# Hybrid encoder block: four of seven low weight parts of each output unit moved from GpSimd to VectorE

## The chip, the cores and the metric

One core of one Trainium2 chip. The metric is device time in microseconds. PE is TensorE (PEld its weight loads), DVE is VectorE, ACT is ScalarE, POOL is GpSimd, SP is the engine that issues most DMAs.

## The reference

One pre-norm mixer layer over x of 1024 tokens by 2048 columns, in float32. One input projection feeds two head groups, whose gated outputs are joined and mixed by one output projection:

```
h = rmsnorm(x, norm_w)
proj = einsum('bsd,de->bse', h, w_in)            # 2048 x 5632
q_a, k_a, v_a, g_a, q_r, k_r, v_r, g_r = split(proj)
attn = windowed_attention(q_a, k_a, v_a)         # +-128 tokens, 16 heads, 4 kv heads
attn = rmsnorm(attn, attn_out_norm_w) * silu(g_a)
ret  = bidirectional_retention(rotary(q_r), rotary(k_r), v_r)    # 8 heads, chunks of 128
ret  = head_groupnorm(ret, ret_gn_w) * silu(g_r)
mixed = concatenate([attn, ret])                 # 1024 x 2048
x = x + einsum('bse,ed->bsd', mixed, w_out)      # 2048 x 2048
return rmsnorm(x, final_norm_w)
```

## The kernel before

**Float32 products from rounded parts.** A float32 operand is held as two parts: `hi`, the value rounded to the matmul's float32r format, and `lo`, the value minus `hi`. Each product takes three matmuls: hi by hi, hi by lo, lo by hi. The helper `split` (L171 to L173) makes the parts: ACT writes `hi` (a rounding copy, L172), then another engine subtracts `hi` from the source (L173, recorded at L166, the line of the helper `tt`). With `G` that engine is POOL.

**Seven products in place of eight.** The output projection is done by the scheme of Strassen and Winograd on blocks. There are 16 output units (`NO`), numbered q = NF to NF + 15, after the NF = 16 units of the input projection that use the same scheme. A unit has seven products p = 0 to 6, each of four steps j with three matmuls of 128 by 512 (`multiply`, L1167 to L1169): 84 matmuls a unit. For these units the stationary operand, the pair `wh` and `wl`, is a 128 by 512 block of the mixed activations, and the moving operand, the rows `h`, is a combination of the output weights.

**Stages of four units.** The four units of a stage (o % 4, o = q - NF) share 28 rows, four for each product. When the last unit of a stage has finished a product, `o_rows` schedules the next stage's four rows for it: SP loads a row (L1035), ACT writes its high half (L1038), DVE its low half (L166, `h<-h`). So the rows change three times while the output units run.

**Raw blocks and sums.** A unit needs four raw blocks `raws[q, 0..3]`, loaded by SP from `xm` (L1133) into eight rotating buffers of tag `r`. `prep_sums` forms the Winograd sums on POOL (L166, `r<-r,r`), four operations a unit: part 0 turns raw block 0 into a difference and makes `sums[q]`, part 1 changes raw block 2, part 2 changes `sums[q]`. `prep(q, p)` then splits the block of a product: p = 0 and 4 take raw block 0, p = 1 block 1, p = 3 block 2, p = 5 block 3, p = 2 and 6 the sum. `wh` and `wl` have three buffers each.

**Order.** In this part each engine runs its instructions in the order of the program. A slot is one product; the slots of neighbouring units interleave as (q,0), (q,1), (q-1,6), (q,2), (q-1,5), (q,3), (q,4). In the middle of slot n, after its step j = 1, `between` calls `prep` for slot n + 2 and then work that was put off (`run_later`). `point`, after every step, issues row loads, row splits, retention steps and the final normalisation. At the end of a slot `o_collect` lets DVE add the product's PSUM bank to an SBUF tile (`e`, `y` or `t` in the profile, L166). The banks: products 0, 2, 5 and 4 of a unit accumulate into one of tag Ma, products 1, 3 and 6 use tag Mb; there are two Ma, two Mb, one O and three ST banks. Tag ST is handed out by `pS()` and `pT()`, which retention's transposes and small matmuls use in turn; the last pair of retention heads is still at work while the first output units run. From stage 2 on ACT squares each finished tile (L1474) and `finish` normalises and stores the rows: a small power on POOL, a few one-column operations on DVE (`newton`), four scalings on DVE (L169).

Of the kernel before, what the change touches and what calls it, by code (L numbers as in the profile page):

```python
# [10 lines left out]
F32R = mybir.dt.float32r  # L11
AF = mybir.ActivationFunctionType
ALU = mybir.AluOpType
# [20 lines left out]
NS, NF = len(STD), len(FAST)  # L34
# [5 lines left out]
def hybrid_block(ctx: ExitStack, tc: tile.TileContext, a: dict, out: bass.AP):  # L40
    nc = tc.nc
    ctx.enter_context(tc.manual_schedule(engines={mybir.EngineType.Pool}))
    V, A, G, T, SP = nc.vector, nc.scalar, nc.gpsimd, nc.tensor, nc.sync
# [94 lines left out]
    def wpair(i):  # L138
        return w_high(), w_low()
# [10 lines left out]
    def psum(tag, bufs):  # L150
        return ps.tile([128, 512], F32, tag=tag, name=nm("ps" + tag), bufs=bufs)

    def pS():
        return psum("ST", 3)
# [10 lines left out]
    def tt(eng, o, x, y, op):  # L165
        eng.tensor_tensor(o, x, y, op)  # L166
# [4 lines left out]
    def split(o_hi, o_lo, x, eng=None):  # L171
        A.copy(o_hi, x)  # L172
        tt(eng or V, o_lo, x, o_hi.bitcast(F32), ALU.subtract)  # L173
# [974 lines left out]
    def prep(q, p):  # L1148
        src = {0: 0, 1: 1, 3: 2, 4: 0, 5: 3}.get(p)
        src = sums[q] if src is None else raws[q, src]  # L1150
        hi, lo = wpair(q)
        split(hi, lo, src, G)
        ready_w[q, p] = (hi, lo)

    def place(q, p, j):
# [133 lines left out]
    for u, (kind, i) in enumerate(STD):  # L1289
# [5 lines left out]
        for pos in range(NK):  # L1295
# [24 lines left out]
            if last_u and pos == 7:  # L1320
                raw_room(0, (2, 0, 3, 1))
                for x in (0, 2, 3, 1):
                    raw_load(0, x)
            elif last_u and pos == 13:
                prep_sums(0, 0)
                prep_sums(0, 1)
            elif last_u and pos in (12, 14):
                prep(*slots[pos // 2 - 6])
            wh, wl = wsp[wi]
            first, last = pos == 0, pos == NK - 1  # L1330
            for b in range(4):
                p = plain[b]
# [56 lines left out]
    for n, (q, p) in enumerate(slots):  # L1389
        slot[0] = n  # L1390
        prepare(q, p, 0)

        def between():
            if n + 2 < len(slots):
                prep(*slots[n + 2])
            run_later()

        if not q:
            rows_done([("c", r) for r in range(4 * p, 4 * p + 4)])
        multiply(q, p, between)  # L1400
        collect(q, p)

        if q == LAST and p < 4:
            for r in range(4 * p, 4 * p + 4):
                todo.append((pt[0] + 2, ("x", r), r, xd[r]))
        if (q, p) == (LAST, 4):
            n_w[0] = W_ALL
            w_load(W_STD)
            w_load(W_STD + 1)
            w_load(W_STD + 2)  # L1410
        elif (q, p) == (LAST, 6):
            w_split(W_STD)
# [91 lines left out]
    def first_slots(w, b):  # L1504
        if (w, b) == (1, 0):
            top[0] = NF + NO
            raw_room(NF, (2, 0, 3, 1))
            for x in (0, 2, 3, 1):
                raw_load(NF, x)
        elif (w, b) == (3, 0):  # L1510
            for x in wanted.pop(-1):
                o_request(*x)
            prep(*oslots[0])
        elif (w, b) == (3, 1):
            prep_sums(NF, 0)
            prep_sums(NF, 1)
        elif (w, b) == (3, 3):
            prep(*oslots[1])

    for u, (kind, i) in enumerate(FAST):  # L1520
# [32 lines left out]
        for w in range(4):  # L1553
# [6 lines left out]
            for b in range(4):  # L1560
                et, hf = b // 2, b % 2
                p = whole[b]
# [159 lines left out]
```

## Time and profile before

| | |
|---|---|
| median of 3 runs | 1531.51 us (1528.52 to 1531.87) |
| profiled execution | 1533.07 us, span 1531.3 us, mean granted TensorE clock 0.994 |
| busy over the span | PE 1463.1, PEld 1218.4, DVE 922.0, ACT 660.4, POOL 844.6 us |
| output units | about 1156 to 1518 us, then 13 us to finish the last rows |
| wl by POOL, from 1156 us | 111 instructions, 1271 / 1300 / 2727 ns (least, median, most) |
| wh by ACT, from 1156 us | 111 instructions, 603 / 622 / 644 ns |
| DMA | 353.18 MB, mean 231 GB/s |

Busy times of different engines overlap. Matmuls are pipelined: one starts every 0.226 us though each is shown with about 0.39 us. A line such as `PE psMa L1168 <- DVE h L166: 7.2, 10, 0.7` reads: PE's instruction at L1168 that writes psMa waited in all 7.2 us, 10 times, at most 0.7 us, for DVE's instruction at L166 that writes h. Buffer numbers are left out of names.

### The profile page before, as it was taken

To read this page: it belongs to the slowest core of one execution; us is meant where nothing else is said; L and a number is where in the kernel's file an instruction comes from. 1 tells how busy PE (TensorE), PEld (TensorE's weight loads), DVE (VectorE), ACT (ScalarE), POOL (GpSimd) and SP (SyncE) were. 2 spreads that over 40 slices of the span, in tenths; PEclk is the share of its full clock that TensorE was granted. 3 is DMA by queue.
4 is the path that set the end of the run, shared out by engine and by line. 5 is a ranking of instruction groups with operands and counts; after the bars stand their busy time and mean duration, and the time that the engine had idled before them with its cause. 6 is when DMAs were issued, how large, how long until landed. Compare 5 with 4: busy or idle time off the path is not lost.

```text
span 1531.3 us, 22172 instructions
## 1 busy us (share of the span) xinstructions
PE 1463.1 (96%) x7250; PEld 1218.4 (80%) x7250; DVE 922.0 (60%) x1791; ACT 660.4 (43%) x1401; POOL 844.6 (55%) x641
## 2 busy tenths in 40 slices
PE   8999998999999999999999999999999998989985
PEld 6998886777888888888788888788887776868764
DVE  5573333864565565565424755754869868483986
ACT  5311133775676675776221232132244243354522
POOL 3232221245546655655666656566446677687863
PEclk9999999999999999999999999999999999999998
DMA  8879889986456456446888589497496586765654
GB/s 304 287 259 337 283 264 314 283 277 203 123 168 162 135 168 186 128 153 208 308 283 268 172 278 355 164 313 271 149 305 240 157 297 217 269 241 182 206 166 144
DMA packets 225072, 353.18 MB, mean 231 GB/s; under 512 B 31883, under 2 KB 86155, under 8 KB 223548
## 3 DMA queue, kind: packets, MB, share of 16 engines
q1 hardware_dynamic: 194492, 330.78, 65.5%
q10 hardware_dynamic: 30464, 20.98, 4.4%
q8 instruction: 57, 0.93, 0.2%
q14 instruction: 59, 0.48, 0.1%
HBM read 239.97 MB, written 124.29 MB: 238 GB/s over the span
## 4 chain that ended last, share of the span: by engine, by line
PE 71%; DMA 9%; DVE 7%; issue 6%; POOL 4%; ACT 2%; SPq 1%; ACTq 0%; DVEq 0%; POOLq 0%
PE psMa L1168 5%; PE psMa L1167 5%; PE psMa L1169 5%; PE psMb L1169 4%; PE psMa L1573 4%; PE psMb L1573 4%; PE psMb L1168 4%; PE psMb L1167 4%; PE psMb L1575 4%; PE psMb L1574 4%; PE psMa L1575 4%; PE psMa L1574 4%; DVE h L166 2%; DMA h<-wc 2%; PE psST L605 2%
## 5 line engine op out<-in xcount | busy, mean ns | idle before, releaser
L166 POOL TENSOR_TENSOR wl<-r,wh 128x512 fp32r<-128x512 f32 x288 | 393.2, 1369 | 400.7 <-ACT wh L172 380.1
L172 ACT CAST wh<-r 128x512 fp32r<-128x512 f32 x288 | 177.5, 619 | 304.2 <-PE psMa L1168 70.8
L1168 PE MATMUL psMa<-h,wh 128*128 128x512 f32 x512 | 201.9, 394 | 7.4 <-DVE h L166 7.2
L1167 PE MATMUL psMa<-h,wh 128*128 128x512 f32 x512 | 203.0, 397 | 4.2 <-DVE t L166 3.5
L1169 PE MATMUL psMa<-h,wl 128*128 128x512 f32 x512 | 200.9, 392 | 0.0
L166 DVE TENSOR_TENSOR h<-h 128x512 fp32r<-128x512 f32 x156 | 174.3, 1146 | 22.9 <-ACT h L1038 22.9
L166 POOL TENSOR_TENSOR r<-r,r 128x512 f32<-128x512 f32 x128 | 182.1, 1423 | 2.8
L166 POOL TENSOR_TENSOR wl<-e,wh 128x512 fp32r<-128x512 f32 x48 | 73.0, 1523 | 199.0 <-ACT wh L172 194.9
L1169 PE MATMUL psMb<-h,wl 128*128 128x512 f32 x384 | 151.4, 394 | 7.9 <-POOL wl L166 7.8
L1167 PE MATMUL psMb<-h,wh 128*128 128x512 f32 x384 | 151.9, 396 | 3.0 <-ACT e L1201 1.7
L1168 PE MATMUL psMb<-h,wh 128*128 128x512 f32 x384 | 150.8, 393 | 2.4 <-DVE h L166 2.3
L166 DVE TENSOR_TENSOR e<-psMa,e 128x512 f32<-128x512 f32 x86 | 58.8, 685 | 106.5 <-PE psMa L1575 79.5
L1168 PEld LDWEIGHTS psMa<-h,wh 128*128 128x128 f32 x512 | 96.6, 189 | 29.4 <-DVE h L166 12.8
L1167 PEld LDWEIGHTS psMa<-h,wh 128*128 128x128 f32 x512 | 96.5, 188 | 23.1 <-issue 3.7
L1169 PEld LDWEIGHTS psMa<-h,wl 128*128 128x128 f32 x512 | 96.5, 189 | 21.0 <-POOL wl L166 0.6
L1573 PE MATMUL psMa<-h,wh 128*128 128x512 f32 x256 | 104.0, 406 | 2.5 <-DVE e L166 2.5
L1573 PE MATMUL psMb<-h,wh 128*128 128x512 f32 x256 | 103.4, 404 | 0.0
L1575 PE MATMUL psMa<-h,wl 128*128 128x512 f32 x256 | 100.0, 391 | 0.0
L1038 ACT CAST h<-h 128x512 fp32r<-128x512 f32 x156 | 90.4, 616 | 22.4 <-DMA h<-cd 9.7
L1575 PE MATMUL psMb<-h,wl 128*128 128x512 f32 x256 | 100.0, 390 | 0.0
L1574 PE MATMUL psMa<-h,wh 128*128 128x512 f32 x256 | 99.8, 390 | 0.0
L1574 PE MATMUL psMb<-h,wh 128*128 128x512 f32 x256 | 99.8, 390 | 0.0
(268 smaller groups left out, 3282.8 us busy)
## 6 DMA issues: line engine op xcount, KB each, us to landing
h<-wc SPq DMA_DIRECT2D x112, 256.0 KB, 5.1
r<-in_w_fast SPq DMA_DIRECT2D x64, 256.0 KB, 3.1
r<-in_w_half SPq DMA_DIRECT2D x64, 256.0 KB, 4.7
h<-in_w_out SPq DMA_DIRECT2D x64, 256.0 KB, 5.0
e<-yd SPq DMA_DIRECT2D x64, 256.0 KB, 4.7
wc<-h SPq DMA_DIRECT2D x64, 256.0 KB, 4.5
r<-xm SPq DMA_DIRECT2D x64, 256.0 KB, 4.1
t<-in_xT SPq DMA_DIRECT2D x31, 512.0 KB, 5.9
```

Source lines behind the costliest of these rows:

```text
L166: eng.tensor_tensor(o, x, y, op)
L172: A.copy(o_hi, x)
L605: T.transpose(p[:, c0], x[:, c0], ident)
L1038: A.copy(rows[r][:, 0:512], rows[r][:, 512:1024].bitcast(F32))
L1167: T.matmul(bank, wh[:, ws], hh, start=(j == 0 and p in (0, 1, 3)), stop=False, skip_group_check=True)
L1168: T.matmul(bank, wh[:, ws], hl, start=False, stop=False, skip_group_check=True)
L1169: T.matmul(bank, wl[:, ws], hh, start=False, stop=(j == 3), skip_group_check=True)
L1573: T.matmul(p, wh[:, ws], hh, start=(w, kk) == (0, 0), stop=False)
L1574: T.matmul(p, wh[:, ws], hl, start=False, stop=False)
L1575: T.matmul(p, wl[:, ws], hh, start=False, stop=last)
```

## The change

In `prep`, for the output units (`q >= NF`) and the products 0, 4, 5 and 6, `split` on POOL is replaced. ACT still writes `hi`; it then writes the same rounded copy once more, into a PSUM bank `c` of tag ST; DVE subtracts `c` from the source and writes `lo`. Products 1, 2 and 3, and all units of the input projection, stay as they were.

```
@@ -1149,7 +1149,14 @@
         src = {0: 0, 1: 1, 3: 2, 4: 0, 5: 3}.get(p)
         src = sums[q] if src is None else raws[q, src]
         hi, lo = wpair(q)
-        split(hi, lo, src, G)
+        if q >= NF and p in (0, 4, 5, 6):
+
+            c = pS()
+            A.copy(hi, src)
+            A.copy(c.bitcast(F32R), src)
+            tt(V, lo, src, c, ALU.subtract)
+        else:
+            split(hi, lo, src, G)
         ready_w[q, p] = (hi, lo)
```

## The prediction

> **What bounds the kernel now.** I read the page first: its head, then the busy times by stage, the waits of TensorE, and the order of time at the places where it waits.
>
> ```profile
> span 1531.3 us, 22172 instructions
> PE 1463.1 (96%) x7250; PEld 1218.4 (80%) x7250; DVE 922.0 (60%) x1791; ACT 660.4 (43%) x1401; POOL 844.6 (55%) x641
> ```
>
> TensorE carries the time. The profiled execution took 1533.07 us, 1.6 us above the median of the runs (1531.51) and 1.8 us above its own span. The edit acts where q >= NF, in the output products, which run from 1156 us to the end. So I cut that part into stages (columns: window, length, busy time and instructions of each engine, clock, DMA share, GB/s).
>
> ```profile
> 1156.00:1250.00 94.00, 88.39 (x438) 72.37 (x437) 72.79 (x140) 36.41 (x72) 62.21 (x50) 0.98 0.62 202
> 1250.00:1292.00 42.00, 37.73 (x157) 28.58 (x156) 41.18 (x39) 19.33 (x35) 33.52 (x22) 1.00 0.78 267
> 1292.00:1330.00 38.00, 38.00 (x169) 31.48 (x168) 10.98 (x16) 10.80 (x18) 28.21 (x23) 1.00 0.69 214
> 1330.00:1372.00 42.00, 37.76 (x161) 29.35 (x160) 40.35 (x40) 22.32 (x43) 32.45 (x21) 1.00 0.79 287
> ...
> 1410.00:1450.00 40.00, 37.12 (x157) 28.58 (x156) 38.55 (x37) 25.70 (x52) 32.34 (x21) 1.00 0.70 243
> 1450.00:1518.00 68.00, 58.01 (x244) 44.53 (x242) 54.26 (x91) 19.56 (x44) 41.04 (x35) 1.00 0.47 151
> 1518.00:1531.00 13.00, 0.00 (x0) 0.00 (x0) 7.05 (x16) 0.72 (x2) 0.55 (x1) 0.64 0.49 162
> ```
>
> The quiet stage 1292 to 1330 is the yardstick: weight loads fill 31.48 of 38 us, 0.828 of the time, one matmul every 38/168 = 0.226 us, with DVE at 29%. Nothing is lost there, so a shorter POOL chain wins nothing there. By the same 0.828 the other stages lose: 1250 to 1292, 42 - 28.58/0.828 = 7.5 us; 1330 to 1372, 6.6; 1410 to 1450, 5.5; 1450 to 1518, 14.2. In the first three DVE is busy 96 to 98% of the time: they are the changes of the rows, when 28 new rows are split by DVE. 1156 to 1250 holds the last retention work, and 1518 to 1531 the last rows' finish, which this edit doesn't touch. The waits of TensorE and of its weight loads from 1156 to 1518 (total us, times, longest):
>
> ```profile
> PE psMa L1168 <- DVE h L166: 7.2, 10, 0.7
> PE psMb L1169 <- POOL wl L166: 6.6, 5, 1.6
> PE psMa L1167 <- DVE t L166: 3.5, 3, 2.0
> ...
> PEld psMa L1168 <- DVE h L166: 12.8, 13, 1.2
> PEld psMb L1169 <- POOL wl L166: 9.7, 7, 2.1
> ```
>
> So the rows' low parts on DVE come last most often, then POOL's low parts of the weights, then banks that DVE empties late.
>
> Why is DVE slow in a row change? The order of time there (start, length, engine):
>
> ```profile
> 1272.43 2.87 DVE L166 TENSOR_TENSOR h<-h 128x512 fp32r<-128x512 f32 x2
> 1275.21 0.68 DVE L166 TENSOR_TENSOR e<-psMb,e 128x512 f32<-128x512 f32 x1
> 1275.82 2.86 DVE L166 TENSOR_TENSOR h<-h 128x512 fp32r<-128x512 f32 x2
> ...
> 1273.32 1.42 POOL L166 TENSOR_TENSOR wl<-r,wh 128x512 fp32r<-128x512 f32 x1 [0.27 <-ACT wh L172]
> 1274.70 3.42 POOL L166 TENSOR_TENSOR r<-r,r 128x512 f32<-128x512 f32 x2
> ...
> 1275.35 0.50 PE L1168 MATMUL psMa<-h,wh 128*128 128x512 f32 x1 [0.73 <-DVE h L166]
> 1277.04 0.50 PE L1168 MATMUL psMa<-h,wh 128*128 128x512 f32 x1 [0.73 <-DVE h L166]
> ```
>
> TensorE moves on by one row every 1.69 us (1275.35 to 1277.04), which is one POOL operation and one DVE subtraction taken in turn. The spread of the durations in 1250 to 1292 (min/median/max ns) shows who suffers:
>
> ```profile
> L166 DVE TENSOR_TENSOR h<-h x26: 674/1604/1781, 1249.2 to 1290.6; 128x512 fp32r<-128x512 f32 x26
> L166 DVE TENSOR_TENSOR e<-psMa,e x7: 673/677/693, 1255.3 to 1291.8; 128x512 f32<-128x512 f32 x7
> L166 POOL TENSOR_TENSOR wl<-r,wh x14: 1291/1594/1782, 1248.9 to 1290.9; 128x512 fp32r<-128x512 f32 x14
> L166 POOL TENSOR_TENSOR r<-r,r x8: 1609/1740/1748, 1250.2 to 1284.0; 128x512 f32<-128x512 f32 x8
> ```
>
> A DVE subtraction with both inputs in SBUF takes 674 ns or up to 1781; one with an input in PSUM takes 673 to 693 whatever POOL does. That asymmetry decides what the change is worth.
>
> **The change part by part.** It takes 4 of 7 wl off POOL in each of 16 units: 64 instructions. It adds 64 copies on ACT into a bank of tag ST and 64 subtractions on DVE with one input in that bank. No DMA is added and no matmul changed.
>
> Prices of the new instructions, from their nearest rows:
>
> ```profile
> L166 DVE TENSOR_TENSOR PTl<-psST,PTh x128: 410/552/560, 266.6 to 705.1; 128x384 fp32r<-128x384 f32 x96, 128x256 fp32r<-128x256 f32 x32
> ...
> L1474 ACT ACTIVATE psO<-y x16: 602/602/604, 1345.6 to 1437.2; 128x512 f32<-128x512 f32 x16
> ...
> L172 ACT CAST wh<-r x111: 603/622/644, 1155.4 to 1508.6; 128x512 fp32r<-128x512 f32 x111
> ```
>
> The subtraction: same operation as PTl at 512 columns, and as e<-psMa at 677 ns; following ones start 0.60 to 0.61 us later (1275.21 to 1275.82), so I take 0.61 us of DVE each. The copy: between 0.60 (into PSUM) and 0.62 us (a cast); I take 0.60. It is 64 x 0.60 = 38 us of ACT, four in 19 us of a unit, hidden by ACT's idle half (19.33 of 42 us in the worst change of rows); without that cover each would delay the next wh by 0.60 us. The Trainium skill's "VectorE: DVE Perf Modes", section on the TRN2 errata, charges a PSUM source 120 cycles of fixed cost against 58, which would make each subtraction 0.065 us dearer than from SBUF and the sum 0.5 us worse per row change; here 677 against 674 ns shows no such step, and the row decides.
>
> *Row changes.* In 1250 to 1292 DVE is busy 41.18 us with 39 instructions that need 39 x 0.61 = 23.8: it waits 17.4 us for 22 POOL operations, 0.79 each. Four sevenths of the 14 wl leave, 8: -6.3. Eight subtractions come: +4.9. Net -1.4 us if waiting shrinks in proportion. The better end: 21 DVE instructions on PSUM (13 + 8, 12.8 us) run beside POOL's remaining 14 x 1.28 = 17.9 us, only 5.1 of which then meets an h: 17.4 - 5.1 - 4.9 = -7.4. The worse end: each new subtraction also waits for its second copy, 8 x 0.60, so +3.4. I take -3, nearer the proportional end because h is still most of DVE's work, and +1 for that waiting: -2 per change, three changes, -6. TensorE follows DVE one for one there, up to the 7.5, 6.6 and 5.5 us that it loses.
>
> *TensorE waiting for wl.* Of the 9.7 us, three waits (near 1344, 1471 and 1495 us, 2.1 + 1.7 + 2.0) stand in the first row of product 6, by the order of banks, and product 6 is moved. Its chain was POOL's sum, one cast, one POOL subtraction of 1.28 us plus queue; it becomes the sum, two casts, 0.61 us of DVE. The sum itself comes earlier, with fewer wl ahead of it on POOL. Ends: 0 (DVE is as late as POOL was) and -5.8; I take -2, since the sums still come from POOL.
>
> *Last stage.* DVE's tiny operations wait for POOL too, and a bank is then emptied late:
>
> ```profile
> 1456.46 1.24 DVE L166 TENSOR_TENSOR ft<-fv,fy 128x1 f32<-128x1 f32 x1 [0.68 <-POOL fy L166]
> 1457.74 1.22 DVE L166 TENSOR_TENSOR ft<-ft,fy 128x1 f32<-128x1 f32 x1
> ...
> 1456.40 2.54 POOL L166 TENSOR_TENSOR wl<-r,wh 128x512 fp32r<-128x512 f32 x2
> ...
> 1460.88 0.47 PE L1167 MATMUL psMa<-h,wh 128*128 128x512 f32 x1 [2.00 <-DVE t L166]
> ```
>
> The two wl at 1456.40 belong to products 4 and 0, both moved: 2 x 1.1 us of DVE waiting goes, 2 x 0.61 comes. DVE has room here (54.26 of 68 us, plus 12 x 0.61 = 7.3). Ends -3.5 (all of this wait) and +3; I take -0.5.
>
> *Retention overlap, 1156 to 1250.* Twelve subtractions, 7.3 us, join a DVE busy 72.79 of 94 us, and the extra bank shares three ST buffers with retention. A dozen wl of POOL leave. One wait stands there that DVE sets:
>
> ```profile
> 1176.13 0.49 PE L812 MATMUL psO<-ST,qs 128*128 128x128 f32 x2 [3.20 <-DVE ST L169]
> ...
> 1177.32 0.63 PE L1168 MATMUL psMa<-h,wh 128*128 128x512 f32 x1
> ...
> 1180.99 0.39 PE L1168 MATMUL psMa<-h,wh 128*128 128x512 f32 x1
> ```
>
> After that wait matmuls last 0.63 instead of 0.39 us for some 3.5 us, about 1.7 us lost. I take 0, ends -4 and +4. "TensorE: Matmul & The Clock Gate" of the Trainium skill, Part 1, says the array falls to half clock after an idle window of about 3.4 us. By that rule a slightly shorter wait here would save those 1.7 us as well, and the sum would be -10.2; the trace agrees that the slowing follows a wait of this size.
>
> *Waits that are added.* DVE's queue is in order. A new subtraction waits for ACT's copy, which stands behind the cast, which waits for its wh buffer; behind the subtraction stand the row splits and bank adds that TensorE waits for. SP is concerned too: it waits for wl before it reloads a raw buffer, and will wait for DVE instead for four of seven.
>
> ```profile
> ACT wh L172 <- PE psMa L1168: 46.6, 25, 5.1
> ...
> SPq L1133 <- POOL wl L166: 71.1, 29, 7.9
> ```
>
> ACT's wait ends when TensorE ends the product before, and DVE's own bank add waits for the same moment, so I expect the extra at one copy or less; SP at nothing, as the new subtraction ends within 0.7 us of the old one's time.
>
> Sum: -6 - 2 - 0.5 + 0 = -8.5 us; on the profiled execution 1533.07 to 1524.6, on the median 1531.5 to 1523.0.
>
> **The rivals.** *DVE's queue is blocked (slower).* Place: the row changes, 24 subtractions. If each holds the row splits behind it for w, the loss is 24 w. From w = 0.35 us it eats the 8.5; at w = 0.60, one copy, 14.4 - 8.5 = +6, so 1537.5. For it: DVE has no idle time there. Against it: rows for a product are put into DVE's queue ahead of the next subtraction, and ACT is half idle.
>
> *An even exchange (no change).* The -1.4 per row change is eaten by the waiting, and product 6 waits for DVE as it did for POOL: 1531. For it: the same DVE is the bound before and after.
>
> *Row changes become TensorE's (much faster).* With the better end of -7.4, capped by the losses, most of 19.6 us comes back, say 16, with 3 + 1 from the other places: 1511.5. For it: PSUM-fed work runs beside POOL untouched.
>
> **How the numbers follow.** Forecast, a gain of 3 to 16 us: 0.48. Much faster: 0.12. Even, within 0.2% (about 3 us, what a measurement of this kernel can tell from no change): 0.17. Slower: 0.23, mostly near 1537. Faster in all: 0.60. The range 1508 to 1538 takes in the two outer cases' centres; the likeliest case alone spans 1515 to 1528.5.
>
> **What would show it.** In the profile after, the median of h<-h at the row changes should fall from 1604 ns to 1300 or less; the new subtractions should last 0.67 to 0.69; TensorE's wait for POOL's wl should shrink from 9.7 us, and DVE's idle time ahead of the new wl stay small. I am wrong if DVE shows long waits for ACT ahead of wl in the row changes, if h<-h stays where it is, or if TensorE's waits for DVE's wl take the place of POOL's.

## The result and the profile after

The changed kernel takes 1520.14 us (median of 4 runs, 1517.61 to 1522.07) against 1531.36 us for the kernel before in the same comparison: ratio 0.993, interval 0.9909 to 0.995. The profiled executions have spans of 1519.2 and 1531.3 us, 12.1 us apart. In the lines below the seven added lines of code have moved line numbers: the three matmuls are L1174 to L1176, the new cast of the high part is L1155 and the copy into PSUM L1156.

The page after, its head and busy times:

```profile
span 1519.2 us, 22187 instructions
PE 1461.1 (96%) x7250; PEld 1219.6 (80%) x7250; DVE 923.3 (61%) x1855; ACT 690.8 (45%) x1465; POOL 751.4 (49%) x577
```

DVE has 64 instructions more and is busy for only 1.3 us more (923.3 against 922.0): its other instructions have become shorter by nearly as much as the new ones take. POOL lost 93.2 us, ACT gained 30.4. The stages (window, length, busy time and instructions of each engine, clock, DMA share, GB/s):

```profile
1156.00:1250.00 94.00, 87.21 (x441) 71.58 (x440) 75.43 (x157) 43.52 (x85) 45.92 (x37) 1.00 0.63 208
1250.00:1292.00 42.00, 41.41 (x179) 32.74 (x178) 38.22 (x48) 24.75 (x45) 22.32 (x15) 1.00 0.80 279
1292.00:1330.00 38.00, 38.00 (x169) 31.48 (x168) 18.08 (x28) 15.18 (x27) 17.62 (x14) 1.00 0.71 243
1330.00:1372.00 42.00, 38.95 (x163) 29.76 (x162) 36.85 (x44) 26.92 (x55) 21.50 (x14) 1.00 0.75 265
...
1410.00:1450.00 40.00, 38.48 (x164) 29.97 (x163) 37.36 (x49) 28.00 (x59) 20.63 (x14) 1.00 0.60 203
```

In the first row change TensorE's weight loads fill 32.74 us instead of 28.58, in the second 29.76 instead of 29.35, in the third 29.97 instead of 28.58. The quiet stage has the same 31.48 as before, as it had nothing to win. By the second row change the changed kernel is 5 us ahead, so that the later windows don't hold quite the same work in both kernels; the table of starts below doesn't have this fault. What the weight loads wait for from 1156 to 1518 us:

```profile
PEld psMa L1175 <- DVE h L166: 10.2, 13, 1.4
PEld psMb L1176 <- DVE wl L166: 3.2, 2, 2.4
...
PEld psMb L1175 <- DVE h L166: 2.4, 5, 0.7
...
PEld psMb L1176 <- POOL wl L166: 1.1, 1, 1.1
...
PEld psMa L1176 <- DVE wl L166: 0.8, 2, 0.6
```

The 9.7 us of waits for POOL's wl are down to 1.1, but 3.2 + 0.8 us of waits for DVE's wl have come. The waits for the rows that DVE splits fell from 12.8 + 5.1 to 10.2 + 2.4.

The first row change in groups, DVE's instructions from 1246 to 1292 us (count, busy us, mean ns). Before:

```profile
L166 DVE TENSOR_TENSOR h<-h 128x512 fp32r<-128x512 f32 x28 | 37.8, 1390 | 0.0
```

After:

```profile
L166 DVE TENSOR_TENSOR h<-h 128x512 fp32r<-128x512 f32 x28 | 27.5, 1006 | 0.0
L166 DVE TENSOR_TENSOR wl<-r,psST 128x512 fp32r<-128x512 f32 x10 | 6.8, 678 | 0.5 <-ACT psST L1156 0.3
```

The same 28 subtractions take 27.5 us instead of 37.8, and the new work costs 6.8: 3.5 us less for DVE. From 1250 to 1292 us the median of h<-h fell from 1604 to 689 ns, and the new subtractions last 671 to 691 ns in the whole part; both are signs that the prediction had named.

Where the time came from, by the start of each product's first low matmul in the two traces, counted from the first output product (all 112 products are in both):

| stretch | before, us | after minus before, us |
|---|---|---|
| units 0 to 3, retention beside them | 94.7 | -0.5 |
| first row change | 44.7 | -4.7 |
| second row change | 44.1 | -0.7 |
| third row change | 40.1 | -1.5 |
| last stage, from product 5 of unit 12 | 60.6 | -4.7 |
| quiet stretches between | | 0.0 |

This compares one trace with one trace. Where two kernels run the same instructions, a stretch still differs by about 1 us: units 0 to 11 of the kernel that changes the last stage alone gave +0.3, -1.1 and -0.2 us in the first three rows. So the -0.5 and the -0.7 can't be told from nothing.

### The profile page after: what moved, and what is told of

Its sections match the earlier page's. It is cut to its first block, busy times and chain, and to the rows that moved or that the text cites. A ratio compares the mean times of both kernels' runs of the same rounds, so it can differ in the third digit from the quotient of the medians.

```text
span 1519.2 us, 22187 instructions
## 1 busy us (share of the span) xinstructions
PE 1461.1 (96%) x7250; PEld 1219.6 (80%) x7250; DVE 923.3 (61%) x1855; ACT 690.8 (45%) x1465; POOL 751.4 (49%) x577
## 4 chain that ended last, share of the span: by engine, by line
PE 67%; DVE 11%; DMA 9%; issue 6%; ACT 3%; POOL 2%; SPq 1%; DVEq 0%; ACTq 0%; POOLq 0%
PE psMa L1175 5%; PE psMa L1176 5%; PE psMa L1174 5%; PE psMb L1176 4%; PE psMb L1175 4%; PE psMb L1174 4%; PE psMa L1580 4%; PE psMb L1580 4%; PE psMa L1582 4%; PE psMa L1581 4%; PE psMb L1581 3%; PE psMb L1582 3%; DVE h L166 3%; PE psST L605 2%; DMA t<-mpd 1%
## 5 line engine op out<-in xcount | busy, mean ns | idle before, releaser
L166 POOL TENSOR_TENSOR wl<-r,wh 128x512 fp32r<-128x512 f32 x224 | 299.2, 1337 | 453.3 <-ACT wh L172 388.1
L172 ACT CAST wh<-r 128x512 fp32r<-128x512 f32 x224 | 138.4, 619 | 216.9 <-PE psMb L1581 62.9
L1174 PE MATMUL psMa<-h,wh 128*128 128x512 f32 x512 | 202.4, 395 | 1.0 <-DVE e L166 0.7
L1176 PE MATMUL psMa<-h,wl 128*128 128x512 f32 x512 | 200.5, 392 | 0.1
L166 DVE TENSOR_TENSOR h<-h 128x512 fp32r<-128x512 f32 x156 | 149.5, 977 | 22.9 <-ACT h L1038 22.9
L1174 PE MATMUL psMb<-h,wh 128*128 128x512 f32 x384 | 152.4, 397 | 3.1 <-ACT e L1208 2.2
L1176 PE MATMUL psMb<-h,wl 128*128 128x512 f32 x384 | 151.5, 395 | 2.9 <-DVE wl L166 2.3
L1175 PEld LDWEIGHTS psMa<-h,wh 128*128 128x128 f32 x512 | 96.4, 188 | 26.9 <-DVE h L166 10.2
L1176 PEld LDWEIGHTS psMa<-h,wl 128*128 128x128 f32 x512 | 96.2, 188 | 21.1 <-DVE wl L166 0.8
L1174 PEld LDWEIGHTS psMa<-h,wh 128*128 128x128 f32 x512 | 96.5, 189 | 19.3 <-ACT wh L172 1.1
```

What stands on the lines that cost most here:

```text
L1174: T.matmul(bank, wh[:, ws], hh, start=(j == 0 and p in (0, 1, 3)), stop=False, skip_group_check=True)
L1175: T.matmul(bank, wh[:, ws], hl, start=False, stop=False, skip_group_check=True)
L1176: T.matmul(bank, wl[:, ws], hh, start=False, stop=(j == 3), skip_group_check=True)
```

## The experiments

Theory 1 is the prediction's: a DVE operation with both inputs in SBUF and a POOL operation exclude each other, and one with an input in PSUM doesn't take part. ("Exclude" means that one has to end before the other goes on.) Theory 2: POOL's queue is shorter, and that is all. The kernel before ran in each of the three groups of experiments; ratios are to it, and gains in us are differences of the medians. Edits are shown against the changed kernel unless the text says otherwise.

**The same work on DVE without PSUM.**

```
         if q >= NF and p in (0, 4, 5, 6):
-            c = pS()
-            A.copy(hi, src)
-            A.copy(c.bitcast(F32R), src)
-            tt(V, lo, src, c, ALU.subtract)
+            split(hi, lo, src, V)
```

> The same 64 low parts go to DVE, but DVE subtracts the high part in SBUF; no second copy, no PSUM bank. Theory 1 (a DVE operation with both inputs in SBUF and a POOL operation exclude each other, one with a PSUM input does not): the new subtractions last up to 1.78 us where POOL works, the median of h<-h in the row changes rises from the changed kernel's 685 ns towards 1.3 us, and at most a third of the changed kernel's gain is left: 1526 to 1531. Theory 2 (POOL's queue is simply shorter, whoever does the work): the gain stays or grows by the saved copies, 1518 to 1521.

Measured: 1527.61 us against 1532.96, ratio 0.9966 (0.9954 to 0.9978). DVE's two groups of subtractions from 1156 to 1518 us (count, busy us, mean ns, idle before):

```profile
L166 DVE TENSOR_TENSOR h<-h 128x512 fp32r<-128x512 f32 x100 | 100.9, 1030 | 0.7 <-ACT h L1038 0.6
L166 DVE TENSOR_TENSOR wl<-r,wh 128x512 fp32r<-128x512 f32 x63 | 55.5, 880 | 5.0 <-ACT wh L172 4.8
```

The changed kernel's group for the same work and window:

```profile
L166 DVE TENSOR_TENSOR wl<-r,psST 128x512 fp32r<-128x512 f32 x63 | 42.9, 681 | 12.8 <-ACT psST L1156 12.3 <-POOL r L166 0.4
```

Neither theory has it all. About half of the gain stays without PSUM (5.4 us, where the changed kernel gained 11.2 and 8.9 in its two comparisons; Theory 1 had allowed a third), so POOL doing less is worth something by itself. By the products' starts of its trace this is not where the prediction had placed the gain: the three row changes won 1.0 us together, where the changed kernel's won 6.8, the last stage 2.6 and the retention overlap 1.5. Some 2 us of the row changes' difference are two stretches in which TensorE ran at half rate (11 matmuls that started every 0.43 in place of 0.226 us). The new subtractions now take 880 ns in the mean (up to 1786) instead of 681: 12.6 us of DVE that the PSUM input saves. The median of h<-h did not rise as I had written; it stayed at 684 ns, and I put that down to POOL's 64 operations, which are gone in this kernel too and can no longer collide with it. That is argued: this kernel doesn't separate a shorter queue of POOL from fewer collisions.

**The copies alone.**

```
-            tt(V, lo, src, c, ALU.subtract)
+            tt(G, lo, src, hi.bitcast(F32), ALU.subtract)
```

> Only the second copy on ACT into a bank of tag ST is added; nothing reads it and POOL still does all low parts. Theory 1: 64 copies of 0.58 us lie in ACT's idle half, 1530 to 1533. Rival (the copies and the shared ST banks delay retention or the next high parts): slower by the 2.6 and 2.4 us that the changed kernel lost in passing in the retention overlap, 1534 to 1537.

Measured: 1532.71 us against 1532.96, ratio 0.9999 (0.9986 to 1.0012). The copies and their banks cost nothing that can be measured, to within about 2 us.

**All seven products.**

```
-        if q >= NF and p in (0, 4, 5, 6):
+        if q >= NF :
```

> All seven products' low parts of the output units go to DVE by a PSUM copy; POOL keeps only the sums. Theory 1: another 48 x 0.61 us on DVE against 48 POOL operations, of which DVE waited 0.79 us each in a row change: a further 0 to 4 us in the row changes, given back in the last stage where DVE has 13 us of idle time in 68: 1515 to 1522. Rival (DVE's queue in order is the limit): DVE's waits for ACT ahead of wl, 12 us in the changed kernel, grow by more than 3/4, TensorE waits for DVE's wl, and the time is above the changed kernel's: 1523 to 1530.

Measured: 1519.05 us against 1532.96, ratio 0.9905 (0.9884 to 0.9927). DVE from 1246 to 1292 us:

```profile
L166 DVE TENSOR_TENSOR h<-h 128x512 fp32r<-128x512 f32 x28 | 23.2, 840 | 0.0
L166 DVE TENSOR_TENSOR wl<-r,psST 128x512 fp32r<-128x512 f32 x17 | 11.6, 680 | 1.6 <-ACT psST L1156 1.5
```

The mean of h<-h goes on falling, 1390, 1006, 840 ns with 0, 4 and 7 products moved, while each new subtraction stays at 680. DVE's wait for ACT ahead of wl rose from 12.3 to 28.7 us. TensorE's weight loads paid a little of that: from 1156 to 1518 us they waited 7.4 us for DVE's wl (4.0 in the changed kernel), but only 6.6 for the rows (12.6). So two signs of the rival (the queue's order as the limit) came, but its price, a time above the changed kernel's, did not.

**The last stage alone.**

```
-        if q >= NF and p in (0, 4, 5, 6):
+        if q >= NF + 12 and p in (0, 4, 5, 6):
```

> The change only in units 12 to 15, the last stage; units 0 to 11 as before. By the starts of the products in the two traces 4.7 us were won from product 5 of unit 12 on and about 1.5 in the third row change. Theory 1: 1525 to 1528. Rival (the last stage won only because it was reached with DVE and SP less late): no gain here, 1530 to 1532.

Measured: 1527.96 us, against 1532.96, ratio 0.9975 (0.996 to 0.999). By the products' starts of its trace the last stage is 4.5 us shorter than in the kernel before. So the last stage wins by itself, and the rival is out.

**The changed kernel again, and product 6 alone.** The first is unaltered; the second is `if q >= NF and p == 6:`.

> The changed kernel unaltered, beside the others of this group: 0.993 of the kernel before, 9 to 12 us less. Whether all seven (14 us less in its own group) are better than four is read against this one.

> Only product 6 of each output unit goes to DVE by a PSUM copy: 16 low parts, not 64. Theory 1 as in the prediction's term: TensorE's three waits in the first row of product 6 (5.8 us) shrink by 2 to 5.8 us, and the row changes give 2/7 of what four products gave: 1526 to 1529. Rival (product 6 waits for POOL's sum, which DVE doesn't make earlier): 1530 to 1533, with the waits near product 6 still there, for DVE's wl instead of POOL's.

Measured: 1522.11 us, ratio 0.9937 (0.9921 to 0.9953), and 1527.01 us, ratio 0.9966 (0.9947 to 0.9985), against 1531.05. Sixteen of the 64 moved parts give 4.0 of the 8.9 us. By the medians product 6 weighs more than its share, which would be 2.2 us, but the interval (2.3 to 8.1 us) hardly excludes that share. The prediction's reading, that its chain begins with POOL's last sum, has no test of its own. The rival, that nothing is won there, is out.

**The rows from PSUM, POOL untouched.** This is the kernel before, with nothing moved off POOL:

```
     def row_low(key, r, src):
         hi, lo = rows[r][:, 0:512], rows[r][:, 512:1024]
-        tt(V, lo, lo.bitcast(F32), hi.bitcast(F32), ALU.subtract)
+        if key[0] == "row" and key[1] >= 1:
+            c = pS()
+            A.copy(c.bitcast(F32R), lo.bitcast(F32))
+            tt(V, lo, lo.bitcast(F32), c, ALU.subtract)
+        else:
+            tt(V, lo, lo.bitcast(F32), hi.bitcast(F32), ALU.subtract)
```

> The kernel before with POOL's work untouched; in the three row changes the low part of each row is taken by DVE from a second rounded copy that ACT writes into a bank of tag ST (84 copies), in place of the high part in SBUF. Theory 1 (exclusion between DVE with two SBUF inputs and POOL): h<-h lasts 0.68 us whatever POOL does, DVE needs 28 x 0.61 + 14 x 0.61 = 26 us of a change of 42, and most of the 7.5 + 6.6 + 5.5 us lost there come back, less what ACT, then 35 of 38 us busy, holds back: 8 to 14 us less, 1518 to 1524. Rival (h<-h was late because POOL's queue delayed the whole chain, not because of the port): no gain, and 84 copies on ACT cost 0 to 5 us.

Measured: 1520.58 us, ratio 0.9926 (0.9909 to 0.9943), 10.5 us less, as Theory 1 had it. POOL's groups from 1246 to 1292 us in the kernel before:

```profile
L166 POOL TENSOR_TENSOR wl<-r,wh 128x512 fp32r<-128x512 f32 x15 | 23.0, 1539 | 11.1 <-ACT wh L172 11.1
L166 POOL TENSOR_TENSOR r<-r,r 128x512 f32<-128x512 f32 x8 | 13.7, 1710 | 0.2
```

POOL's and the rows' groups here, in the same window:

```profile
L166 POOL TENSOR_TENSOR wl<-r,wh 128x512 fp32r<-128x512 f32 x17 | 21.9, 1296 | 12.9 <-ACT wh L172 9.7 <-PE psMb L1173 1.8 <-DMA h<-wc 1.4
L166 DVE TENSOR_TENSOR h<-h,psST 128x512 fp32r<-128x512 f32 x28 | 18.8, 683 | 8.7 <-ACT psST L1044 8.7
...
L166 POOL TENSOR_TENSOR r<-r,r 128x512 f32<-128x512 f32 x10 | 13.0, 1295 | 0.2
```

POOL does 27 operations here, and yet h<-h takes 683 ns in the mean instead of 1390, and POOL's two groups take 1296 and 1295 instead of 1539 and 1710. Both engines stop paying for each other as soon as DVE reads one input from PSUM. That is Theory 1 shown by itself, with the work of POOL unchanged.

**Both together.** All seven products and all rows from PSUM:

> All seven low parts by DVE from PSUM and the rows of the three changes too. Theory 1: DVE's waits for POOL vanish from both sides; the row changes then have 28 + 14 + 14 DVE operations of 0.61 us, 34 us, and ACT 28 + 14 + 14 + 28 casts and copies, 50 us for two units of 38: ACT becomes the bound there, about 10 us a change lost, and the time is no better than all seven alone: 1517 to 1530. Rival (ACT's copies overlap enough): 1505 to 1512.

Measured: 1535.8 us, ratio 1.0024 (1.0012 to 1.0036): 4.8 us above the kernel before. ACT's order of time in the first row change:

```profile
1264.84 0.61 ACT L1160 CAST wh<-r 128x512 fp32r<-128x512 f32 x1
1265.37 0.57 ACT L1161 CAST psST<-r 128x512 fp32r<-128x512 f32 x1
1265.88 0.61 ACT L1038 CAST h<-h 128x512 fp32r<-128x512 f32 x1
1266.40 0.58 ACT L1044 CAST psST<-h 128x512 fp32r<-128x512 f32 x1
1266.93 0.61 ACT L1038 CAST h<-h 128x512 fp32r<-128x512 f32 x1
1267.45 0.58 ACT L1044 CAST psST<-h 128x512 fp32r<-128x512 f32 x1
1267.97 0.61 ACT L1160 CAST wh<-r 128x512 fp32r<-128x512 f32 x1
```

One operation every 0.52 us with no gap, six for a product: 1264.84 to 1267.97, 3.13 us, where TensorE needs 2.72. ACT has become the bound, and DVE waits for it (17.8 us ahead of wl and 16.9 us ahead of the rows, 1246 to 1450 us). From the first output product's start to the last one's the trace has 357.8 us, where the rows alone had 343.1 and the seven products alone 341.5: together, the two gains are gone. But 357.8 is only 0.2 us more than the 357.6 of the kernel before. The other 5.5 us by which its profiled execution is longer lie ahead of the first output product, in work that the edit leaves alone, where the kept traces differ by up to 8 us (first starts from 1154.1 to 1162.2). So ACT explains why nothing is won; why the median is higher than before is not shown.

**A mixture, and half of the rows.** The first keeps all rows from PSUM, with product 6 from unit 3 and all products from unit 13 on (`if q >= NF + 13 or q >= NF + 3 and p == 6:`). The second is the changed kernel with every second row from PSUM (`key[1] >= 1 and key[3] % 2`, the last entry being the step j).

> A version made from the results: in the three row changes DVE takes every row's low part from a PSUM copy (84 copies, as in the rows' experiment); product 6 goes to DVE from unit 3 on and all seven products from unit 13 on, after the last row change, where ACT has room; all other low parts stay on POOL. Theory 1: the rows' gain of 11.3 us, plus 3 to 5 us in the last stage and 1 to 2 at product 6: 1513 to 1518. Rival (the gains overlap, or ACT, at 37 of 46 us in a row change, has no room for product 6): 1519 to 1523.

> The changed kernel (products 0, 4, 5, 6 on DVE from PSUM) and in the row changes the low parts of every second row from a PSUM copy (42 copies). With ACT stepping every 0.52 us and a product every 2.72 us, ACT has room for 5.2 operations a product; this asks 1 + 4/7 + 2 + 1 = 4.6, where rows and all seven asked 6. Theory 1 (ACT's step decides what of the port's loss can be won back): the row changes lose little, 6 to 9 us less than the changed kernel: 1513 to 1517. Rival (in-order waits between ACT and DVE decide, not ACT's sum): 1520 to 1530.

Measured: the mixture 1519.61 us, ratio 0.9916 (0.9891 to 0.9941), above what Theory 1 had asked and inside the rival's range. By the products' starts it won 6.2, 1.6 and 0.0 us in the three row changes, where the rows alone won 6.5, 3.2 and 2.5, and 3.7 instead of 1.9 in the last stage: what the moved products gave at the end they cost in the row changes. That ACT, with more copies there, is the cause is argued, not tested, and some 1.4 us of the third row change's 2.5 are a stretch of seven matmuls at half rate (1431.0 to 1433.5 us), which the rows alone don't have. Half of the rows: 1515.1 us against 1530.61, ratio 0.9887 (0.986 to 0.9913), as forecast from ACT's step, and by the medians the fastest kernel of all; its ratio lies wholly below that of the changed kernel beside its experiments (0.9921 to 0.9953). Its first row change is as full as the quiet stage (1246 to 1292 us):

```profile
1246.00:1292.00 46.00, 46.00 (x204) 37.92 (x203) 36.94 (x56) 35.63 (x67) 22.52 (x16) 1.00 0.85 296
```

37.92/46 = 0.824, against 0.828 in the yardstick.

**Without the retention overlap.** `if q >= NF + 3 and p in (0, 4, 5, 6):`

> The changed kernel, but units 0 to 2, which run beside the last retention work, as before (POOL, no PSUM copy). The prediction priced this stretch at 0 with ends of -4 and +4; the traces give -0.5 us there, after 2.7 and 3.1 us of passing loss. If the stretch is worth nothing: the changed kernel's time, 1519 to 1523. If the three ST banks shared with retention cost: 1516 to 1518. If the stretch won: 1524 or more.

Measured: 1522.39 us, ratio 0.9941 (0.9919 to 0.9963), the time of the changed kernel. The overlap is worth nothing that can be measured, either way.

## Why the prediction came out

It forecast 1523.0 us, 8.5 less on the median, and the kernel came 11.2 us lower. The forecast's mechanism holds; its terms came out unevenly, and the term for the last stage was too small. Step by step:

*Row changes, -6 taken (-2 each; ends -7.4 and +3.4).* Measured -4.7, -0.7 and -1.5, together -6.8; in the second trace of the changed kernel -4.7, +1.6 and -1.5. The mechanism was right and is shown by the rows' experiment; the sum was close, but not its even spread, so that part of its closeness is luck. The +1 us of each change for DVE's waiting was too dear: DVE waited 0.3, 1.5 and 0.3 us for ACT ahead of wl. In the second row change the four new rows of product 4 still meet POOL's sums, which were not moved:

```profile
1352.03 2.86 DVE L166 TENSOR_TENSOR h<-h 128x512 fp32r<-128x512 f32 x2
...
1350.91 3.42 POOL L166 TENSOR_TENSOR r<-r,r 128x512 f32<-128x512 f32 x2
...
1353.25 0.50 PE L1175 MATMUL psMa<-h,wh 128*128 128x512 f32 x1 [0.73 <-DVE h L166]
1354.94 0.50 PE L1175 MATMUL psMa<-h,wh 128*128 128x512 f32 x1 [0.73 <-DVE h L166]
```

The step is 1.69 us again, one POOL operation and one row in turn. The +1.6 of the second trace has a further reason: there these waits are followed by twelve matmuls at half rate (1355.3 to 1360.0 us, one every 0.43 us in place of 0.226), about 2.4 us, while the first trace has none in this place.

*Waits for wl, -2, and the last stage, -0.5.* These were too small. The last stage alone won 4.7 us in the trace. Of this, 2.2 us were won at product 4 of unit 13, where the prediction had shown TensorE waiting 2.00 us for `t` and had named -3.5 as the better end. POOL's waits went as thought, and in part DVE's came in their place at product 6, as the even rival had it; the fence shows TensorE waiting for DVE, which is at work on the normalisation:

```profile
1459.48 2.53 DVE L169 SCALAR_TENSOR_TENSOR y<-y,fy,fw 128x512 f32<-128x512 f32 x2
1461.93 0.68 DVE L166 TENSOR_TENSOR e<-psMa,e 128x512 f32<-128x512 f32 x1
1462.53 0.67 DVE L166 TENSOR_TENSOR wl<-r,psST 128x512 fp32r<-128x512 f32 x1
...
1463.26 0.50 PE L1176 MATMUL psMb<-h,wl 128*128 128x512 f32 x1 [1.99 <-DVE wl L166]
1463.60 0.48 PE L1174 MATMUL psMb<-h,wh 128*128 128x512 f32 x1
1463.88 0.63 PE L1175 MATMUL psMb<-h,wh 128*128 128x512 f32 x1
1464.31 0.63 PE L1176 MATMUL psMb<-h,wl 128*128 128x512 f32 x1
```

Seven matmuls at half rate follow (the granted clock is 0.60 from 1464 to 1468 us, against 1.00 in the kernel before), and from product 4 of unit 13 to product 2 of unit 14 the 2.2 us were lost again. Product 6 of unit 14 then won 1.9.

What I had not counted: product 1 stays on POOL and still won 2.1 us at its start in unit 15. POOL's queue was not the reason. In the kernel before, POOL stood idle for 1.48 us there, behind a cast that waited for its raw block:

```profile
1483.76 0.48 SPq L1133 DMA_DIRECT2D r<-xm  x1
...
1488.64 1.14 ACT L172 CAST wh<-r 128x512 fp32r<-128x512 f32 x2 [3.21 <-DMA r<-xm]
...
1489.33 1.69 POOL L166 TENSOR_TENSOR wl<-r,wh 128x512 fp32r<-128x512 f32 x1 [1.48 <-ACT wh L172]
...
1491.08 0.50 PE L1169 MATMUL psMb<-h,wl 128*128 128x512 f32 x1 [1.04 <-POOL wl L166]
```

And in the changed kernel:

```profile
1473.78 0.51 SPq L1133 DMA_DIRECT2D r<-xm  x1
...
1478.51 0.62 ACT L172 CAST wh<-r 128x512 fp32r<-128x512 f32 x1 [2.99 <-DMA r<-xm]
```

The load was issued 2.5 us ahead of product 0's first low matmul in the kernel before (at 1486.25 us) and 4.8 us ahead of it in the changed kernel (at 1478.62), where TensorE no longer waits. The prediction had put SP at nothing; here an earlier load was worth up to 2.1 us. Why SP came to it earlier is not settled. In the kernel without the PSUM input the last stage won 2.6 us, and nothing at this product. How the 4.7 us divide between load, queue and port is not settled further.

*Retention overlap, 0 (ends -4 and +4).* Measured -0.5, and nothing in the kernel that leaves it out. In passing it lost 2.7 us at the fourth product, where TensorE's small matmuls into a bank of tag ST waited 2.4 us for DVE's `sd`, and had it back by product 0 of unit 1; it then lost 3.1 us up to product 0 of unit 2 and won that back within unit 2. The half rate that the prediction had seen at 1177 us is gone (the granted clock from 1176 to 1180 us is 1.00, where it was 0.61; the wait ahead of it is 1.92 us instead of 3.20). So the 1.7 us of the prediction's sum of -10.2 were saved, but other waits took most of them.

*The copies, nothing.* Right by their own experiment. A copy took 582 ns (median), 0.60 had been taken.

*The queue-order rival.* It needed 0.35 us for each new subtraction. DVE waited 12.3 us for 64 of them:

```profile
DVE wl L166 <- ACT psST L1156: 12.3, 22, 2.1
```

That is 0.19 us each over the whole part. In the windows of the three row changes it was 0.3, 1.5 and 0.3 us for 26 subtractions, 0.08 us each. In another kernel, with six operations for a product, another engine did become the bound: ACT.

## What to carry to other kernels

When DVE operations of one shape last either one length or more than twice that, list what POOL does at the same moments before blaming a queue: here one PSUM input in place of SBUF freed both engines, with the same work on each. Such a copy is paid by the engine that writes PSUM, so count its operations per step of the bound engine; some four and a half per product in the row changes won 15.5 us here, five (the rows alone) 10.5, six nothing. And try the product that stands last in a chain of sums by itself: a quarter of the moved work gave 4.0 of 8.9 us, by medians whose interval is wide.

## What the runs showed of the chip that I had not expected

ACT's copies from SBUF follow one another every 0.52 us, whether into SBUF (0.61 to 0.62 us shown) or into PSUM (0.57 to 0.58 us shown), so that the second copy costs what the first does. And the exclusion is mutual: POOL's subtractions of 1.59 us (median, first row change) fall to 1.30 when the rows' inputs no longer both lie in SBUF.

The length of a single wait doesn't tell whether TensorE then runs at half rate. In the changed kernel's trace a wait of 1.99 us was followed by seven matmuls that started every 0.43 us (at 1463.26 us, shown above), and waits of 2.38 us (at 1170.74) and 1.92 us (at 1177.44) were followed by none. What decides it is not shown here. The output products of the fastest kernel have no such stretch.
